# Where the latent attention starts beside the context's chain of work

## The chip, the cores and the metric

The kernel runs on one core of one Trainium2 chip. The metric is the device time of one execution, in microseconds (us). Five engines run side by side, each with its own instruction queue that is worked off in order: TensorE (PE, the matmuls; its weight loads are shown as PEld), VectorE (DVE), ScalarE (ACT), GpSimd (POOL) and SyncE (SP), which here issues nearly all DMAs.

## The reference

Two layers of a diffusion backbone work on 1024 latent tokens and 256 context tokens of width 1024. Layer 0 mixes by a short gated convolution and by differential attention, then applies one output projection; each layer ends in a gated ConvFFN. Context tokens read only context, latent tokens read both. What matters here is the second half of layer 0, cut to its core:

```python
y_lat = finish(gates_l, o_lat)                       # o_lat: attention of 1024 latent queries over 1280 keys
y_ctx = finish(gates_c, diff_attend(qc, kc, vc, lam))  # finish: concat(conv, attention) @ w_out
ctx = ctx + g1c * y_ctx                              # the context's output projection
ctx = ctx + g2c * conv_ffn(modulate(rms_norm(ctx, norm2_g[i]), sh2c, sc2c), ...)
```

`diff_attend` makes two softmax maps per head over the keys, subtracts the second times a factor from the first, and multiplies by v; the result is RMS-normalised per head. The context's output projection, norm and FFN need only context data; the latent attention needs q, k and v of layer 0. Neither needs the other.

## The kernel before

All matmuls of the gemm kind are done as three passes (high by high, high by low, low by high part) in `mm3` (lines 217 to 219). Weights come through `WStream`: a DMA into `wr`, a cast on ACT into `wh` (line 112), a subtraction on DVE into `wl` (line 114).

`attention` (line 1252 on) runs two generators side by side. The first, `chain`, is the context's tail of layer 0: one step that loads the mixed features (`mraw`, line 686) and splits them into `s4c`; eight steps of the output projection (PSUM tile `po`, 24 matmuls of 256 columns each, then `xc += gate * po` on DVE, line 696); two steps of `norm`; 22 `u` steps of the FFN's upper half (PSUM `pab`); and 24 `d` steps of its lower half (PSUM `pd`). The second, `att_lat`, is the latent attention: 4 heads by 2 halves of 512 queries make 8 blocks (`AttBlock`), numbered b0 to b7 below, of 4 query tiles each (q0 to q3). A query tile is three pieces: `scores` (twice, once per softmax map: six matmuls into the PSUM tile `S`, a maximum on DVE at line 1472, an exponential on ACT at line 1474 that reads `S`), `combine` (line 1487), and `product` (transposes `tpp`, line 1504, copies to `pth` and `ptl`, and for every second query tile the matmuls `pv`, whose result is written to `osq` and `osb`, lines 1514 and 1515). Two later pieces close a block: `stats` (column sums of `osq`, PSUM `ost`) and `out` (broadcast, `osb` scaled at line 1533 and stored at line 1534). `S` has one buffer, the PSUM tag `w` of `tpp`, `pv`, `ost` and `orb` two, the tag `mm` of the chain three.

`weave` takes steps of both generators in proportion to their planned number of steps. This gives the order of the program text. A planner then puts every engine's instructions into its queue ahead of the run: it goes by the order of the text where two instructions are ready, takes a later one where the earlier is not, and hands out the buffers of a tag when the tile is first written.

The tag `t2k` of the pool `tmp` (4 buffers of 512 columns) is shared by `mraw`, by the norm and by the attention:

```python
self.tmp = Pool(ctx.enter_context(tc.tile_pool(name="tmp", bufs=1)), {"t2k": ("t2k", 4)})
# norm, for k in range(8): squares; the first two stay as the two running sums
s = tmp.tile([P, 512], F32, tag="t2k", name="sq")[:, :T]
nc.scalar.activation(s, xk(k), AF.Square)
# norm, for k in range(8): the normed tile
t = keep(k) if keep else tmp.tile([P, 512], F32, tag="t2k", name="nt")[:, :T]
# AttBlock.__init__: both live until the block's `stats` and `out`
self.sq = net.tmp.tile([P, 512], F32, tag="t2k", name="osq")[:, :Q]
self.o = net.tmp.tile([P, 512], F32, tag="t2k", name="osb")[:, :Q]
```

`att_lat` makes the tiles of b0 at its start and those of block n+1 after `combine` of q2 of block n. The norm's squares are at lines 383 to 389, its column sum `st` at line 370, its reciprocal root at lines 357 and 359, its normed tiles `nt` at line 402.

Of the kernel before, what the change touches and what calls it, by code (L numbers as in the profile page):

```python
# [84 lines left out]
def weave(*gens):  # L85

    live = [[g, n, 0] for g, n in gens]
    while live:
        e = min(live, key=lambda e: (e[2] + 0.5) / e[1])
        if next(e[0], StopIteration) is StopIteration:  # L90
            live.remove(e)
        e[2] += 1
# [44 lines left out]
class Net:  # L137
# [1114 lines left out]
    def attention(self):  # L1252

        nc, tc, I = self.nc, self.tc, self.I
        B = self.modB
        with ExitStack() as s:
            cp = s.enter_context(tc.tile_pool(name="cp", bufs=1, reuse_waits="tile"))
            ap = s.enter_context(tc.tile_pool(name="ap", bufs=1, reuse_waits="tile"))
            pp = s.enter_context(tc.tile_pool(name="psS", bufs=1, space=PSUM, reuse_waits="tile"))
            xc = cp.tile([P, 8, CTX], F32, name="xc")  # L1260
            xk = lambda k: xc[:, k, :]
            s4c = lambda: cp.tile([P, 2, CTX], F32R, tag="s4c", name="s4c", bufs=14)
            tmp = self.tmp
            ps = Pool(pp, {"mm": ("mm", 3), "tp": ("mm", 3), "st": ("mm", 3)})

            def chain():
                op = self.out_proj(xk, CTX, SEQ, 1, self.mix, s4c, tmp, ps, lambda m, v: B[:, m, v:v + 1])
                next(op)
                nc.sync.dma_start(xc, I["ctxT"])
                yield  # L1270
                yield from op
                hs = []
                yield from self.norm(xk, CTX, self.gs[(0, 2, 1)], lambda k: B[:, 8 + k, 1:2], s4c, tmp, ps, hs, True)
                big = Pool(cp, {"a": ("a", 2), "b": ("b", 1), "cv": ("cv", 2), "e": ("e", 1)})
                yield from self.ffn(0, xk, CTX, hs, 4, s4c, big, ps, lambda m: B[:, 24 + m, 1:2])
                nc.sync.dma_start(self.xcD, xc)

            at = Pool(ap, {t: (t, 2) for t in ("k0", "k1", "vh", "vl", "qa0", "qa1", "qb0", "qb1", "s1", "p0", "p1",
                                               "e1", "r1")})
            pw = Pool(pp, {"w": ("w", 2), "S": ("S", 1)})  # L1280
            ch = chain()
            for _ in range(11):
                next(ch)
            weave((ch, 9 + 2 + 22 + 6 * 4 - 11), (self.att_lat(at, pw), 68))

    def rest(self, stop=99):
        nc, tc, I, O = self.nc, self.tc, self.I, self.O
# [364 lines left out]
```

## Time and profile before

| what | value |
|---|---|
| time, median of 3 runs | 2654.31 us (2648.61 to 2654.5) |
| the profiled execution: its own time | 2658.96 us |
| its span | 2657.2 us |
| PE busy | 2551.8 us, 96% of the span |
| DVE busy | 1947.5 us, 73% |
| ACT busy | 1166.3 us, 44% |
| granted TensorE clock, mean over the span | 0.974 |

Busy time of an engine is the union of its instructions. A matmul's row lasts longer than the time until the next one may start, because matmuls are pipelined: what a matmul takes of PE is read from start to start. A row of the timeline gives the start, the busy time, engine, line, operation, tiles and count, and in brackets the idle time just before it with what ended it. The granted clock is 1.00 at 2.4 GHz and 0.50 at 1.2 GHz.

### The profile page before, as it was taken

How to read it: one execution, taken by the hardware profiler on the slowest of the kernel's cores; microseconds unless marked ns; L12 is line 12 of the kernel's file. 1: busy time of each engine (PE TensorE's matmuls, PEld its weight loads, DVE VectorE, ACT ScalarE, POOL GpSimd, SP SyncE). 2: the span in 40 equal slices, each digit the busy share in tenths (PEclk: the TensorE clock that was granted, in tenths of full speed). 3: DMA queues.
4: the chain of work that ended last, by engine and by line, in shares of the span. 5: the costliest groups of instructions: out<-in, count | busy, mean ns of one | idle time of the engine just before them, and what ended most of it. 6: DMA issues, size and time to landing. Idle time of an engine off the chain costs nothing.

```text
span 2657.2 us, 34664 instructions
## 1 busy us (share of the span) xinstructions
PE 2551.8 (96%) x12666; PEld 2145.4 (81%) x12666; DVE 1947.5 (73%) x3077; ACT 1166.3 (44%) x1751; POOL 241.4 (9%) x321
## 2 busy tenths in 40 slices
PE   6999998999998998999999998999899999999999
PEld 6777887999997886888888886877688788888887
DVE  7467965999997587777778978446558766666984
ACT  5322324767675354444443454133235444444442
POOL 3221000000000041000000002013203100000000
PEclk6999999999999999999999999999799999999999
DMA  7224545443433624434458664577662222225874
GB/s 257 93 95 135 182 135 165 134 143 112 124 116 111 232 65 149 134 127 133 130 178 302 218 206 141 177 232 222 191 217 72 103 88 80 87 80 202 281 242 139
DMA packets 209547, 414.01 MB, mean 156 GB/s; under 512 B 20320, under 2 KB 89568, under 8 KB 208992
## 3 DMA queue, kind: packets, MB, share of 16 engines
q1 hardware_dynamic: 206352, 406.41, 46.6%
q10 hardware_dynamic: 3024, 5.38, 0.6%
q8 instruction: 99, 1.62, 0.3%
q14 instruction: 72, 0.59, 0.1%
HBM read 341.98 MB, written 69.73 MB: 155 GB/s over the span
## 4 chain that ended last, share of the span: by engine, by line
PE 63%; DVE 13%; issue 12%; DMA 7%; ACT 3%; POOL 2%; SPq 0%; ACTq 0%; DVEq 0%; POOLq 0%
PE PA L217 4%; PE PA L218 4%; PE PA L219 4%; PE pd L218 3%; PE pd L219 3%; PE pd L217 3%; PE PB L217 2%; PE PB L218 2%; PE PB L219 2%; PE pt L217 2%; PE pt L218 2%; PE pt L219 2%; PE po L218 2%; PE po L217 2%; PE po L219 2%
## 5 line engine op out<-in xcount | busy, mean ns | idle before, releaser
L114 DVE TENSOR_TENSOR wl<-wr,wh 128x1024 fp32r<-128x1024 f32 x254 | 309.6, 1221 | 178.4 <-ACT wh L112 176.1
L112 ACT CAST wh<-wr 128x1024 fp32r<-128x1024 f32 x254 | 261.9, 1034 | 394.1 <-PE PA L218 67.3
L217 PE MATMUL pd<-s,wh 128*128 128x512 f32 x616 | 241.2, 392 | 4.9 <-ACT s L963 4.9
L218 PE MATMUL pd<-s,wh 128*128 128x512 f32 x616 | 241.4, 392 | 1.8 <-DVE s L964 1.8
L219 PE MATMUL pd<-s,wl 128*128 128x512 f32 x616 | 241.1, 391 | 0.0
L217 PE MATMUL PA<-s,wh 128*128 128x512 f32 x544 | 212.2, 390 | 0.2 <-DVE a L893 0.2
L219 PE MATMUL PA<-s,wl 128*128 128x512 f32 x544 | 211.8, 389 | 0.0
L218 PE MATMUL PA<-s,wh 128*128 128x512 f32 x544 | 211.8, 389 | 0.0
L351 DVE SCALAR_TENSOR_TENSOR mw<-mw,cr 128x256 f32<-128x256 f32 x256 | 111.4, 458 | 81.3 <-DMA mw<-in_mod1T 71.9
L112 ACT CAST wh<-r 128x1024 fp32r<-128x1024 f32 x80 | 67.0, 837 | 220.6 <-PE PB L218 126.5
L217 PEld LDWEIGHTS pd<-s,wh 128*128 128x128 f32 x616 | 116.4, 189 | 29.4 <-ACT s L963 5.3
L218 PEld LDWEIGHTS pd<-s,wh 128*128 128x128 f32 x616 | 116.4, 189 | 27.2 <-DVE s L964 3.2
L219 PEld LDWEIGHTS pd<-s,wl 128*128 128x128 f32 x616 | 116.4, 189 | 24.2
L217 PE MATMUL PB<-s,wh 128*128 128x512 f32 x320 | 125.0, 390 | 1.2 <-ACT p L889 1.2
L218 PE MATMUL PB<-s,wh 128*128 128x512 f32 x320 | 124.8, 390 | 0.0
L219 PE MATMUL PB<-s,wl 128*128 128x512 f32 x320 | 124.6, 389 | 0.0
L217 PEld LDWEIGHTS PA<-s,wh 128*128 128x128 f32 x544 | 102.2, 188 | 22.3 <-DVE a L893 1.3
L219 PEld LDWEIGHTS PA<-s,wl 128*128 128x128 f32 x544 | 102.1, 188 | 21.2
L218 PEld LDWEIGHTS PA<-s,wh 128*128 128x128 f32 x544 | 102.2, 188 | 21.1
L1474 ACT ACTIVATE p<-S,s 128x1280 f32<-128x1280 f32 (+1 forms) x80 | 92.9, 1161 | 52.7 <-DVE s L1472 51.2
L359 POOL TENSOR_TENSOR rr<-vv,mhalf 128x8 f32<-128x8 f32 (+2 forms) x39 | 57.6, 1478 | 587.8 <-DVE vv L357 563.3
L1472 DVE TENSOR_REDUCE s<-S 128x1 f32<-128x1280 f32 (+1 forms) x80 | 102.0, 1275 | 11.1 <-PE S L1471 10.1
(385 smaller groups left out, 7000.3 us busy)
## 6 DMA issues: line engine op xcount, KB each, us to landing
wr<-in_w_up SPq DMA_DIRECT2D x98, 512.0 KB, 3.4
wr<-in_w_dn SPq DMA_DIRECT2D x92, 512.0 KB, 4.3
gr<-gD SPq DMA_DIRECT2D x154, 256.0 KB, 3.7
mw<-in_mod1T SPq DMA_DIRECT2D x256, 128.0 KB, 3.2
gD<-fcv SPq DMA_DIRECT2D x44, 512.0 KB, 3.6
wr<-in_w_out SPq DMA_DIRECT2D x40, 512.0 KB, 4.2
r<-in_w_up SPq DMA_DIRECT2D x40, 512.0 KB, 3.3
mbw<-in_mod0T SPq DMA_DIRECT2D x32, 512.0 KB, 3.6
```

What stands on the lines that cost most here:

```text
L112: self.nc.scalar.copy(hi, raw)
L114: eng.tensor_tensor(lo, raw, hi.bitcast(F32), op=ALU.subtract)
L217: mm(out, L[0], R[0], start=first, stop=False)
L218: mm(out, L[0], R[1], start=False, stop=False)
L219: self.last_mm = mm(out, L[1], R[0], start=False, stop=last)
L351: self.nc.vector.scalar_tensor_tensor(w, in0=w, scalar=1.0, in1=c, op0=ALU.mult, op1=ALU.mult, accum_out=d)
L359: self.last_pow = nc.gpsimd.tensor_tensor(r, vv, self.mhalf[:, :n], op=ALU.pow)
L1472: nc.vector.tensor_reduce(s2[:, m:m + 1], sv, axis=AX.X, op=ALU.max, negate=True)
L1474: nc.scalar.activation(e, sv, AF.Exp, bias=s2[:, m:m + 1], accum_out=self.s1[:, qt:qt + 1] if m == 0 else s2[:, 2:3])
```

## The change

The chain is no longer advanced by eleven steps (load, eight steps of output projection, two of the norm) before the weave begins, but by one (the load). The other ten steps become part of the weave, whose planned number of chain steps goes from 46 to 56. No instruction is added or removed.

```diff
             ch = chain()
-            for _ in range(11):
-                next(ch)
-            weave((ch, 9 + 2 + 22 + 6 * 4 - 11), (self.att_lat(at, pw), 68))
+            next(ch)
+            weave((ch, 9 + 2 + 22 + 6 * 4 - 1), (self.att_lat(at, pw), 68))
```

The order of the text that `weave` makes, by its rule (the generator whose next step lies earliest, (done + 0.5) / planned), begins as follows; A is a piece of the attention, C a step of the chain:

```
before: C load, C po0..po7, C norm1, C norm2, A scores b0q0, C u0, A combine b0q0, C u1, A scores b0q1, ...
        ... C u3, A product b0q1 + combine b0q2 + tiles of b1, A scores b0q3, C u4, ...
after:  C load, A scores b0q0, C po0, A combine b0q0, C po1, A scores b0q1, C po2, ...
        ... C po4, A product b0q1 + combine b0q2 + tiles of b1, A scores b0q3, C po5, ...
        ... C po7, A product b0q3 + combine b1q0, C norm1, A scores b1q1, A stats b0, C norm2, A scores b1q2, C u0,
        A out b0 + product b1q0 + product b1q1 + combine b1q2 + tiles of b2, C u1, ...
end, before: ... C d16-3, A scores b7q2, C u21, A out b6 ..., A scores b7q3, C d20-0, ...
end, after:  ... C d16-3, A out b6 ..., A scores b7q3, C u21, A combine b7q3, C d20-0, ...
```

## Rows read from the trace of the kernel before

**Rows 1.** The page, part 1: busy time, share of the span, instructions.
```profile
PE 2551.8 (96%) x12666; PEld 2145.4 (81%) x12666; DVE 1947.5 (73%) x3077; ACT 1166.3 (44%) x1751; POOL 241.4 (9%) x321
```
**Rows 2.** Windows, 425 to 862 us: stretch, length, busy by engine, clock, DMA.
```profile
425.00:450.00 25.00, 23.82 (x194) 23.56 (x195) 15.96 (x28) 12.43 (x24) 0.00 (x0) 1.00 0.79 208
450.00:475.00 25.00, 13.14 (x56) 10.78 (x55) 22.33 (x31) 16.22 (x26) 4.29 (x5) 0.59 0.57 171
...
480.00:800.00 320.00, 316.70 (x2428) 301.58 (x2427) 303.52 (x446) 224.31 (x391) 13.17 (x46) 1.00 0.40 124
820.00:850.00 30.00, 21.12 (x152) 18.83 (x150) 26.88 (x43) 17.57 (x31) 0.00 (x0) 0.98 0.25 90
850.00:862.00 12.00, 10.46 (x48) 8.96 (x47) 3.73 (x8) 2.76 (x6) 1.01 (x1) 0.64 0.61 206
```
**Rows 3.** Timeline of PE: output projection, norm, first FFN matmul.
```profile
425.51 0.62 PE L217 MATMUL po<-s4c,wh 128*128 128x256 f32 x3 [1.21 <-ACT s4c L688]
...
449.45 0.28 PE L219 MATMUL po<-s4c,wl 128*128 128x256 f32 x1
...
457.06 1.02 PE L370 MATMUL st<-ones,sq 128*128 128x1 f32 x4 [6.17 <-DVE sq L389]
...
466.41 0.79 PE L1470 MATMUL S<-k,qa 128*128 128x512 f32 x1 [5.57 <-ACT p L1474]
467.27 0.58 PE L217 MATMUL pab<-s4c,wh 128*128 128x256 f32 x1
```
**Rows 4.** Timeline of ACT: exponentials of b7, little chain work left.
```profile
823.56 1.34 ACT L1474 ACTIVATE p<-S,s 128x1280 f32<-128x1280 f32 x1
...
828.03 1.33 ACT L1474 ACTIVATE p<-S,s 128x1280 f32<-128x1280 f32 x1 [0.94 <-DVE s L1472]
...
843.00 1.33 ACT L1474 ACTIVATE p<-S,s 128x1280 f32<-128x1280 f32 x1
```
**Rows 5.** Timeline of PE: matmuls of one query tile.
```profile
836.65 0.33 PE L217 MATMUL pv<-pth,vh 128*128 128x256 f32 x1
...
840.12 0.39 PE L1470 MATMUL S<-k,qa 128*128 128x512 f32 x1
...
841.27 1.03 PE L1504 MATMUL tpp<-ident,p 128*128 128x128 f32 x8
```
**Rows 6.** Tile sq in 420:470, and timeline of DVE: the norm.
```profile
L383 ACT ACTIVATE sq<-xc x8: 405/414/418, 435.0 to 453.4; 128x256 f32<-128x256 f32 x8
L388 DVE TENSOR_TENSOR sq<-sq x6: 416/418/427, 437.1 to 455.1; 128x256 f32<-128x256 f32 x6
...
456.58 0.42 DVE L389 TENSOR_TENSOR sq<-sq 128x256 f32<-128x256 f32 x1
```
**Rows 7.** Timelines of ACT and SP, tile osb: the end of block b7.
```profile
856.49 0.38 ACT L1514 ACTIVATE osq<-pv 128x256 f32<-128x256 f32 x1 [5.70 <-PE pv L219]
...
860.85 0.33 SPq L1534 DMA_DIRECT2D mix<-osb  x1
...
DMA to landing us min/median/max: 1.7/2.1/3.6
```
**Rows 8.** Timeline of SP, tile kraw, timeline of DVE: the first head.
```profile
429.10 1.09 SPq L666 DMA_DIRECT2D kraw<-kT  x2
...
DMA to landing us min/median/max: 3.8/4.9/7.4
...
438.77 1.49 DVE L669 TENSOR_TENSOR k<-kraw,k 64x1280 fp32r<-64x1280 f32 x1
```
**Rows 9.** Timeline of PE at the end of the attention.
```profile
847.26 1.06 PE L1504 MATMUL tpp<-ident,p 128*128 128x128 f32 x8 [2.26 <-DVE p L1487]
```
**Rows 10.** Timeline of SP before the output projection: its first loads.
```profile
360.12 0.33 SPq L1534 DMA_DIRECT2D mix<-osb  x1
...
371.33 10.04 SPq L588 DMA_DIRECT2D mix<-cv  x2
...
382.89 8.39 SPq L686 DMA_DIRECT2D mraw<-mix  x3
```

## The prediction

> **What bounds the kernel now.** I read the page first: PE is busy for 2551.8 of 2657.2 us, DVE for 1947.5 [rows 1]. A busy PE can still be a waiting one, so the second view is the windows over the stage that the change touches, 425 to 862 us. From 480 to 800 us, where attention and FFN are woven, PE is busy for 316.70 of 320 us at the full clock, and DVE for 303.52 [rows 2]. PE idles 3.3 us there, 1%, so this stretch ends when PE's work ends; DVE at 95% has little room, but it is second. The two ends are different. From 425 to 475 us PE idles 1.2 + 11.9 = 13.1 us, and the granted clock falls to 0.59 in the second half [rows 2]. From 820 to 850 us PE idles 8.9 us while DVE is busy for 26.88 of 30 [rows 2].
>
> Third, PE's timeline shows what the first hole is. The eight output projections run without a hole from 425.51 to 449.45 us; then PE waits 6.17 us for the norm's sum and 5.57 us for the first exponentials, and the first FFN matmul starts at 467.27 [rows 3]. A matmul of S already stands in this hole: the planner pulls the attention's start forward by itself. The hole costs more than its idle time. A mean clock of 0.59 over 25 us means that some 20 us ran at the 1.2 GHz level; of the 13.14 us that PE worked in this half about 10 lay in it and at full clock would have taken 5. So the opening costs 13.1 + 5 = 18 us of PE time. That is all that the change can win there.
>
> **The change part by part.** No instruction comes or goes, on any queue. What moves is the attention against ten steps of the chain, and the DMAs that they issue: kraw, qraw and vraw of b0 and b1 are now ahead, on SP, of the weights of the later output projections. In the trace the first kraw goes out at 429.10, right behind the mraw loads, and its landing takes 3.8 to 7.4 us [rows 8]. It can hardly go earlier, because the mraw loads stay first. With 4.9 us of landing, the cast, and 1.49 us for the split on DVE [rows 8], S of b0q0 starts near 438 instead of 449.6, and b0q1's first exponential, after the second key tile has gone through the single kraw buffer, near 452. What is pushed back on SP is weights, 0.3 us each in the queue and prefetched two ahead; I cost it at nothing, and with that cover gone at one landing, for which kraw's 4.9 us is the nearest row [rows 8].
>
> The output projection is 192 matmuls in 449.45 - 425.51 = 23.9 us [rows 3]. It now shares PE with about one and a half query tiles and is through near 455.
>
> **The step that decides is the norm's buffers.** The tag t2k has four. The text now has b0's osq and osb, then b1's, then the norm's eight squares, its eight nt, and then b2's. I take it that a tag's buffers are given in the order of the text, a later tile never before an earlier one. The trace bears this out weakly: after the last block but one of the context's attention is stored at 360.12, SP has spare time, yet the first mraw loads go out only at 382.89 [rows 10], when the last block's osq and osb, earlier in the text, are about to be written. If it holds, the squares wait until b1's osq and osb have been given, at b1q1's product. The first two squares then take b0's buffers and stay there as the running sums, so the third square waits until `stats` of b1 has read osq. Until then the whole chain stands still: no FFN, and only attention on PE.
>
> How long? Alone, the attention goes at the pace of the one S buffer: reduce, exponential, next matmuls. Exponentials at 823.56 and 828.03 are 4.47 us apart; over four half tiles to 843.00 it is 19.44 / 4 = 4.86 [rows 4]. I take 4.7, so 9.4 us for a query tile. From b0q1's first exponential at 452 to b1q3's second are 13 half tiles, 61 us: 513. From the last exponential to the written osq the end of b7 took 856.49 - 843.00 = 13.5 us [rows 4, 7]; with part of that at the low clock I take 13: 526. Six squares through one free buffer, each 0.41 us on ACT and 0.42 on DVE [rows 6], some 0.95 with the hand-overs: 6 us, 532. From the last sum at 456.58 to the first FFN matmul at 467.27 are 10.7 us [rows 3, 6]: 543. osb of b1, stored 4.4 us after osq and landed 2.1 us later [rows 7], comes inside that. b2's osq needs a buffer only at about 545, so no second wait follows.
>
> So PE has attention alone from 455 to 543, 88 us. One query tile takes 2 x (841.27 - 840.12) = 2.3 us for S, 10 transposes at 1.03 / 8, 1.3 us with their tail (1.1 without), half of 840.12 - 836.65 for pv, 1.7 [rows 5], and 0.3 for a quarter of a block's sums and broadcasts: 5.4 to 5.6, I take 5.4. PE then idles 88 x (1 - 5.4 / 9.4) = 37 us. The lower bound takes 4.47 a half tile and a start 6 us earlier, 75 us: 75 x (1 - 5.4 / 8.9) = 29. The upper takes 4.86 and a start later by 4, 95 us: 95 x (1 - 5.4 / 9.7) = 42. At the opening itself the 1.2 us stays. I expect no low clock in this stretch, as the mean clock was 0.98 from 820 to 850 us with holes of this kind [rows 2].
>
> Against 18 - 1 = 17 us lost before at this place, 37 us are 20 more, with the bounds 12 to 25. Afterwards the chain is behind and is served first; PE stays full, as it was, and DVE has slightly less than before per unit of PE work, so nothing is lost there; won is at best the 1% of the stretch that PE idles now, 3 us, at least 0. I take 2, as the chain's matmuls are always ready while it is behind.
>
> At the end of the weave u21 comes two places later, beside b7q3's combine. Its 48 matmuls of 256 columns take 48 x 0.125 = 6 us, from 23.9 / 192 a piece [rows 3], and can fall into PE's holes there: 8.9 us in 820 to 850, and such a one as the 2.26 us ahead of b7q3's transposes [rows 2, 9]. I take 5 of the 6 as won; bounds 0 and 6.
>
> Sum: +20 for the stall against the old hole, -5 for the end, -2 for the catching up: +13 us on the profiled execution's 2658.96 (its span and 1.8 us around it), which is 4.65 above the median of the runs. On the median: 2654.31 + 13 = 2667 us. With the bounds, 12 - 6 - 3 = +3 and 25 us, so the likeliest's own range is 2658 to 2679.
>
> The Trainium skill (Perfetto Trace Analysis, Optimization Strategy) says that a kernel with several regimes may gain when they are interleaved; by that alone the change would win the opening's idle time, the case of the first rival. The same section says that the same gap repeating on the engine that should be saturated can mean that there is no SBUF for the next tile. No run here shows such a stretch yet: PE idles 1% of 480 to 800 us [rows 2].
>
> **The rivals.** First, on the other side: the squares get buffers when their data is there, whatever the text says, and b0's osq waits a little instead. Then the norm ends near 475 with attention beside it, PE loses some 8 us in place of 18 (the 1.2 at the start, one wait of the 6.17 kind cut to half, and some low clock), and u21 wins 3 of its 6: 2654 - 10 - 3 = 2641, or 2635 to 2648. For it: the planner moves ready work ahead, as the S matmul in the norm's hole shows [rows 3]. Against: mraw's late start [rows 10]. It decides if the squares' first rows on ACT stand before b1's first osq. Chance 0.16.
>
> Second, the change does not do what it says: the planner already starts the attention at 429.10 as soon as it can [rows 8], so the queues hardly change and so does the time, 2654. Against: the squares' wait follows from the text, not from readiness. It also covers a stall whose 29 us are nearly met by 18 + 7 won. Chance 0.14.
>
> Third, the stall also lowers the clock: PE idles 43% of it, and in the opening 12 us of idle time in 25 were enough for a clock of 0.59 [rows 2]. At half rate S takes 1.15 us more per half tile, 8 query tiles 18 us more: 2685. Against: 0.98 from 820 to 850 us, with 30% idle [rows 2]. Chance 0.10.
>
> **How the numbers follow.** Forecast 0.60, rivals 0.16, 0.14, 0.10. A measurement of this kernel tells about 0.3%, 8 us, from no change. Of the forecast 0.46 lies above +8 us and 0.14 below; the first rival gives 0.14 faster and 0.02 same, the second 0.12 same and 0.01 on either side, the third 0.10 slower. Together slower 0.57, same 0.28, faster 0.15. The range runs from 2641, the middle of the first rival, to 2682, leaving out half of it, most of the third and the forecast's tails, under 2 in 10.
>
> **What would show it.** Right: S of b0q0 some 10 us earlier; the squares, now done by 453.4 [rows 6], in two groups, the third after b1's first ost matmuls, past 500; the first pab near 543 instead of 467; from 455 to 543 PE busy near 57%, with a clock of 1.00; four query tiles more done at 543 than before; fewer idle us on PE in the last 40 us of the weave. Wrong: the first pab before 490 (first rival), the order on PE unchanged (second), a clock well under 1 between 455 and 543 (third), or PE idle time in the later weave well over 1%, which would mean that the catching up is not free.

## The result: 1% slower, and the profile after

| | before | after |
|---|---|---|
| time, median | 2654.25 us (2648.61 to 2654.5, 4 runs) | 2680.18 us (2670.85 to 2682.11, 4 runs) |
| the profiled execution: its time, span | 2658.96, 2657.2 us | 2680.5, 2678.6 us |

The ratio is 1.0096, 95% interval 1.0069 to 1.0123: 18 to 33 us slower. The forecast said 2667, so the sign was right, the time lies inside the range, and the loss is twice the one forecast. From the line of `exp` on, lines of the kernel after have numbers one lower than before (L1473 for L1474).

Part 1 of the page, for [rows 1]:

```profile
PE 2558.1 (96%) x12666; PEld 2150.0 (80%) x12666; DVE 1948.8 (73%) x3077; ACT 1165.5 (44%) x1751; POOL 236.4 (9%) x321
```

The counts are the same, so nothing was added. PE is busy 6.3 us longer for the same matmuls, and the span grew by 21.4. To see where, take the stage from the first matmul of the context's output projection to the first of the latent one, which is the same work in both kernels. The windows of before over that stage (stretch, length, busy time of PE, PEld, DVE, ACT, POOL, clock, DMA):

```profile
425.50:859.70 434.20, 407.93 (x3063) 386.52 (x3063) 391.60 (x576) 288.02 (x497) 20.38 (x53) 0.97 0.42 130
425.50:480.00 54.50, 41.96 (x290) 39.34 (x291) 41.44 (x62) 31.16 (x52) 4.29 (x5) 0.81 0.69 194
...
800.00:859.70 59.70, 49.26 (x349) 45.60 (x347) 46.65 (x70) 32.55 (x55) 2.92 (x2) 0.94 0.32 107
```

And of after:

```profile
426.40:888.00 461.60, 419.71 (x3062) 393.67 (x3063) 395.23 (x576) 287.33 (x497) 15.16 (x53) 0.94 0.40 123
426.40:550.00 123.60, 91.62 (x576) 82.04 (x577) 91.91 (x129) 68.92 (x116) 5.08 (x10) 0.81 0.41 118
...
450.00:475.00 25.00, 13.53 (x58) 10.60 (x57) 20.80 (x23) 13.37 (x18) 0.00 (x0) 0.71 0.72 204
475.00:500.00 25.00, 18.18 (x104) 15.28 (x103) 20.46 (x25) 14.27 (x25) 0.00 (x0) 0.81 0.29 81
500.00:525.00 25.00, 11.98 (x52) 9.51 (x51) 16.09 (x30) 11.92 (x25) 4.05 (x5) 0.60 0.00 1
525.00:550.00 25.00, 25.00 (x189) 24.30 (x188) 17.77 (x28) 16.72 (x31) 1.03 (x6) 0.92 0.29 95
550.00:820.00 270.00, 268.06 (x2063) 255.28 (x2061) 249.48 (x365) 182.91 (x320) 7.99 (x41) 1.00 0.41 126
...
820.00:888.00 68.00, 60.04 (x429) 56.34 (x428) 53.83 (x84) 35.50 (x64) 2.09 (x4) 0.92 0.35 117
```

The stage is 461.6 - 434.2 = 27.4 us longer: 41.9 us of idle PE instead of 26.3, which is 15.6, and 419.7 us of busy PE instead of 407.9 for the same 3063 matmuls, which is 11.8. Most of the second part is the clock. A mean of 0.94 over 461.6 us is about 55 us at the half level; 0.97 over 434.2 was about 26. Added up over the stretches at 0.50, PE is busy for 36 us of them in after and for 17 in before; at the full clock this work would take half, so the clock accounts for about 9.5 of the 11.8 us. This is an estimate, and the other 2 us are not traced. The loss lies in the opening; from 550 to 820 us PE idles 1.9 us of 270, less than the 3.3 of 320 in [rows 2]. This stage's 27.4 fits the 26 us between the medians. The profiled spans differ by only 21.4, because outside the stage, where both kernels do the same, the profiled execution of before took 6.0 us longer; its time is 4.7 us above its own median.

PE's timeline in the opening, for [rows 3] (start, busy time, ..., in brackets the idle time ahead and what ended it):

```profile
426.40 0.61 PE L217 MATMUL po<-s4c,wh 128*128 128x256 f32 x3 [1.22 <-ACT s4c L688]
...
452.65 0.28 PE L219 MATMUL po<-s4c,wl 128*128 128x256 f32 x1
...
502.75 0.95 PE L370 MATMUL ost<-ones,osq 128*128 128x1 f32 x8
...
516.33 1.02 PE L370 MATMUL st<-ones,sq 128*128 128x1 f32 x4 [1.92 <-DVE sq L389]
518.37 0.69 PE L375 MATMUL rb<-ident,rr 128*128 128x128 f32 x2 [1.03 <-POOL rr L359]
...
522.86 0.79 PE L217 MATMUL pab<-s4c,wh 128*128 128x256 f32 x2 [3.81 <-ACT s4c L413]
...
532.21 0.60 PE L375 MATMUL orb<-ident,r 128*128 128x128 f32 x4
```

The projection ends 3.2 us later than before, as it shares PE. The first FFN matmul comes at 522.86 instead of 467.27: 70 us behind the last projection matmul, where it was 18. ACT's timeline, for [rows 6], shows why:

```profile
442.89 1.33 ACT L1473 ACTIVATE p<-S,s 128x1280 f32<-128x1280 f32 x1 [1.72 <-DVE s L1471]
...
453.87 1.32 ACT L1473 ACTIVATE p<-S,s 128x1280 f32<-128x1280 f32 x1
...
459.54 1.32 ACT L1473 ACTIVATE p<-S,s 128x1280 f32<-128x1280 f32 x1
...
482.63 0.47 ACT L1514 ACTIVATE osb<-pv,subg 128x256 f32<-128x256 f32 x1
482.99 0.72 ACT L383 ACTIVATE sq<-xc 128x256 f32<-128x256 f32 x2
...
503.79 0.42 ACT L383 ACTIVATE sq<-xc 128x256 f32<-128x256 f32 x1 [1.26 <-PE ost L370]
...
510.44 1.33 ACT L1473 ACTIVATE p<-S,s 128x1280 f32<-128x1280 f32 x1 [2.00 <-DVE s L1471]
...
512.68 0.42 ACT L383 ACTIVATE sq<-xc 128x256 f32<-128x256 f32 x1 [0.51 <-DVE sq L388]
...
536.41 1.31 ACT L1473 ACTIVATE p<-S,s 128x1280 f32<-128x1280 f32 x1
```

Not one square of the norm runs until b0's `osb` has been written at 482.63; then two run in the same microsecond, and the third stands until `ost` of b0 has read `osq`. The bracket names that reader. That is a wait for a buffer: the squares' data was there, since the last projection ended at 452.65. The rows also show something else: the exponentials stop for 26 us between 510.44 and 536.41.

What ended PE's idle time in this stretch, by groups of lines from 450 to 525 us (count, busy us and mean ns, idle time ahead and its releasers):

```profile
L1469 PE MATMUL S<-k,qa 128*128 128x512 f32 (+1 forms) x33 | 16.7, 505 | 16.3 <-ACT p L1473 16.2
L1503 PE MATMUL tpp<-ident,p 128*128 128x128 f32 x40 | 8.3, 354 | 7.1 <-DVE ptl L1505 4.1 <-DVE p L1486 3.0
...
L217 PE MATMUL pab<-s4c,wh 128*128 128x256 f32 x3 | 1.2, 470 | 3.8 <-ACT s4c L413 3.8
```

Of 31 us, 16.3 are S waiting for the exponential that frees its buffer and 7.1 the transposes: attention alone on PE, limited by its own circle over DVE and ACT. The cause of the stall does not stand in this table. It shows what is left to do for PE while the chain is kept out, and the missing work has no row.

At the end ([rows 7]), ACT's timeline has b7's `osq` at 884.89 instead of 856.49:

```profile
884.89 0.38 ACT L1513 ACTIVATE osq<-pv 128x256 f32<-128x256 f32 x1 [5.53 <-PE pv L219]
```

### The profile page after: what moved, and what is told of

It reads as the page before. It is cut to its first block, busy times and chain, and to the rows that moved or that the text cites. A ratio compares the mean times of both kernels' runs of the same rounds, so it can differ in the third digit from the quotient of the medians.

```text
span 2678.6 us, 34650 instructions
## 1 busy us (share of the span) xinstructions
PE 2558.1 (96%) x12666; PEld 2150.0 (80%) x12666; DVE 1948.8 (73%) x3077; ACT 1165.5 (44%) x1751; POOL 236.4 (9%) x321
## 4 chain that ended last, share of the span: by engine, by line
PE 62%; DVE 13%; issue 12%; DMA 7%; ACT 4%; POOL 2%; ACTq 0%; SPq 0%; DVEq 0%; POOLq 0%
PE PA L218 4%; PE PA L217 4%; PE PA L219 4%; PE pd L218 3%; PE pd L219 3%; PE pd L217 3%; PE PB L217 2%; PE PB L218 2%; PE PB L219 2%; PE pt L217 2%; PE pt L219 2%; PE pt L218 2%; PE po L218 2%; PE po L217 2%; PE po L219 2%
## 5 line engine op out<-in xcount | busy, mean ns | idle before, releaser
L218 PEld LDWEIGHTS pd<-s,wh 128*128 128x128 f32 x616 | 116.3, 189 | 26.3 <-DVE s L964 2.2
L1473 ACT ACTIVATE p<-S,s 128x1280 f32<-128x1280 f32 (+1 forms) x80 | 92.8, 1160 | 67.5 <-DVE s L1471 65.0
L219 PEld LDWEIGHTS PA<-s,wl 128*128 128x128 f32 x544 | 102.1, 188 | 21.1
```

What stands on the lines that cost most here:

```text
L218: mm(out, L[0], R[1], start=False, stop=False)
L219: self.last_mm = mm(out, L[1], R[0], start=False, stop=last)
L1473: nc.scalar.activation(e, sv, AF.Exp, bias=s2[:, m:m + 1], accum_out=self.s1[:, qt:qt + 1] if m == 0 else s2[:, 2:3])
```

## The experiments

The theory: the chain is kept out by the four `t2k` buffers, that is all, and with buffers of its own the change would win what it looked for. The rival that came from the trace: the order ties do it as well. `in_order` (line 362) issues the norm's and the attention's small matmuls (`st`, `rb`, `ost`, `orb`) behind the last gemm matmul that stands ahead of them in the text. With the chain woven in, that is a matmul of the other generator.

Line numbers in a run's rows are those of its own kernel. In each entry the time behind "against" is that of the kernel before, measured beside the run. The stage is the time from the first context `po` to the first latent `po` in the profiled execution, as above: 434.2 us before, 461.6 after. A single execution of it tells no difference of 5 us: the two controls below, as fast as before by their medians, have 436.4 (c1) and 439.5 (c2).

**Own buffers for the norm (e1_own).** The pool of the chain gets two more `cv` buffers, which the norm uses ahead of the FFN; a small class `NormTmp`, not shown, turns the norm's tag `t2k` into this one. Control c1_before_own: the same edit in the kernel before.

```diff
-  yield from self.norm(xk, CTX, ..., s4c, tmp, ps, hs, True)
-  big = Pool(cp, {..., "cv": ("cv", 2), ...})
+  yield from self.norm(xk, CTX, ..., s4c, NormTmp(cp, tmp), ps, hs, True)
+  big = Pool(cp, {..., "cv": ("cv", 4), ...})
```

> Theory (buffers): the change loses because the norm's squares wait for the four t2k buffers behind b0's osq and osb. With four buffers of the chain's own for the norm, the squares are done before 465 us, the first pab starts before 490 instead of 523, PE idles under 15 us from 450 to 525 (changed kernel: some 31), and the time is 2635 to 2650 us, below before's 2654. Rival (order): what costs is that the attention's loads and DVE work now lie ahead of the projections' weights, whatever the buffers; then the time stays at 2670 to 2682 us.

> Control: the kernel before, with the norm's own buffers. By the theory (buffers) the norm never waits there, since it ends ahead of b0's osq: 2651 to 2657 us. If four buffers for the FFN's tile of the same tag, or the other addresses, were a gain in themselves, it would be 5 us or more faster, and the first run would have to be read against it.

Measured: 2671.34 us (6 runs) against 2659.12, ratio 1.0052 (1.0034 to 1.0070); stage 450.4. Control 2658.86, 0.9996 (0.9985 to 1.0007). So the buffers are part of the loss and not the whole of it; the theory alone falls: `pab` comes at 512.3 and not before 490. The time lies in the range of the rival (order), which e4 below takes up. What is left stands in the answer for the tile `sq` of e1 (count, shortest, median and longest ns, first and last start):

```profile
L395 ACT ACTIVATE sq<-xc x8: 407/418/419, 438.1 to 459.6; 128x256 f32<-128x256 f32 x8
...
L401 DVE TENSOR_TENSOR sq<-sq x1: 405/405/405, 470.5 to 470.5; 128x256 f32<-128x256 f32 x1
```

And in PE's timeline of e1:

```profile
504.75 0.28 PE L231 MATMUL pv<-pth,vl 128*128 128x256 f32 x1
504.87 0.50 PE L382 MATMUL st<-ones,sq 128*128 128x1 f32 x4
...
512.33 0.79 PE L229 MATMUL pab<-s4c,wh 128*128 128x256 f32 x2 [1.18 <-ACT s4c L425]
```

All eight squares are through by 460 and the sum is complete at 470.9, yet its column sum `st` runs at 504.87, directly behind the last `pv` of b0q3, with no idle time between. b0q3's product stands ahead of the norm in the text, and `st` is tied to its last matmul. A second wait had stood behind the first, 34 us long.

**The tie of the attention's own sums taken away (e2_free), and both (e3_both).** `stats` and `out` issue their matmuls without `in_order` (the edit in `stats`; `out` has its counterpart, not shown):

```diff
-  net.colsum(st, self.sq, n)
+  for j in range(n):
+      nc.tensor.matmul(st[:, j:j + 1], self.sq[:, j * P:(j + 1) * P], net.ones, start=True, stop=True)
```

> The attention's sums and broadcasts (ost, orb) are no longer tied behind the last gemm matmul of the text. Theory (tie): in the changed kernel b0's orb waits behind u0 of the stalled chain, and with it the PSUM tag w, so that the attention stands still from 511 to 535 us too; without the tie its exponentials go on through 511 to 535 and the time falls by 6 to 12 us to 2668 to 2674, the first pab staying near 523. Rival (buffers alone): the attention stands still because of the buffers of t2k; then the gap of 26 us between two exponentials stays and the time stays at 2676 to 2682 us.

> Both edits together. If the buffers are the root and the tie only carries the stall on, this stands within 4 us of the run with the norm's own buffers alone (2635 to 2650 us). If the tie costs something of its own all along the weave, it is 5 us or more below that run. If the order of loads is what costs, it stays above 2665.

Measured: e2 2683.29 us (4 runs), 1.0100 (1.0079 to 1.0121), stage 460.0; e3 2671.84 (7 runs), 1.0046 (1.0030 to 1.0062), stage 445.8. The expected gain of e2 is a miss. e3 stands with e1 and not at 2635 to 2650; above 2665, it too leaves the order of the loads open. PE's timeline of e2:

```profile
509.13 1.11 PE L1533 MATMUL orb<-ident,r 128*128 128x128 f32 x4 [2.40 <-POOL r L1527]
```

And the exponentials in ACT's, from 507 to 532 us:

```profile
507.61 1.33 ACT L1473 ACTIVATE p<-S,s 128x1280 f32<-128x1280 f32 x1 [0.37 <-DVE s L1471]
...
514.68 1.33 ACT L1473 ACTIVATE p<-S,s 128x1280 f32<-128x1280 f32 x1
...
522.82 1.33 ACT L1473 ACTIVATE p<-S,s 128x1280 f32<-128x1280 f32 x1
...
530.78 1.33 ACT L1473 ACTIVATE p<-S,s 128x1280 f32<-128x1280 f32 x1 [0.44 <-DVE s L1471]
```

Here the exponentials go on to 530.8, since `orb` no longer waits behind the FFN's first gemm; the stop from 510 to 536 in after came from this tie. It cost nothing, though: without it `pab` comes at 528.9, 6 us later than in after, and once the chain is free PE is full with or without attention.

**Own buffers and no tie at all (e4_own_untied), no tie alone (e5_untied).** Within `attention()` `in_order` gives no edge. Control c2_before_own_untied: both edits in the kernel before.

```diff
-  return self.tc.issue_after(self.last_mm.ins) if self.last_mm else nullcontext()
+  return self.tc.issue_after(self.last_mm.ins) if self.last_mm and self.tie else nullcontext()
...
+  n.tie = False
   n.attention()
+  n.tie = True
```

> The norm's own buffers, and no tie to the last gemm matmul of the text in attention and chain during the weave. Theory (two waits): with own buffers the squares were done at 460 us, but the column sum st came at 505, because it is tied behind the last matmul of the text, b0q3's pv. Without the tie st comes before 475, the first pab before 490, PE idles under 15 us from 450 to 525 and the time is 2635 to 2654 us, not slower than before. Rival (order): the attention beside the projections costs by itself, in the weave and at its end; then st and pab come early and the time still stays at 2662 us or more.

> The changed kernel without the tie alone, t2k still shared. Theory (two waits): the third square still waits for b0's osq to be read, near 503 us, so the stall stays: first pab at 515 to 530, time 2674 to 2686 us. If the tie were the only wait that counts, the first pab would come before 490 and the time fall below 2660.

> Control: the kernel before with the norm's own buffers and without the tie. Both theories: the norm's sum follows the projections there anyway, so 2651 to 2662 us, within 4 us of before in the same call. If it were 6 us or more faster, a gain of the untied version with the change would belong to the tie, not to the place of the attention.

Measured: e4 2660.92 us (12 runs) against 2656.94, 1.0009 (0.9998 to 1.0019), stage 438.1; e5 2681.58 (6 runs), 1.0090 (1.0073 to 1.0107), stage 455.6; control 2657.32, 1.0003 (0.9991 to 1.0014). Without the tie but with shared buffers the loss is that of after: the third square still waits for `ost` (ACT's timeline of e5):

```profile
505.34 0.42 ACT L384 ACTIVATE sq<-xc 128x256 f32<-128x256 f32 x1 [1.25 <-PE ost L371]
```

With both waits away the loss is gone but for at most 5 us, by the interval of e4. `st` before 475 and `pab` before 490 came as expected; the time came neither in the theory's range (up to 2654) nor in the rival's (from 2662), so the order of the text can still cost a little, and it is not what cost the 26 us. So there are two waits in series. The buffer's ends later: taking it alone away wins some 12 us, taking the tie alone away nothing that these runs tell, and only both win it, within those 5 us. Nothing is won over before either. PE's timeline of e4:

```profile
467.59 0.50 PE L383 MATMUL st<-ones,sq 128*128 128x1 f32 x4
...
483.35 0.50 PE L230 MATMUL pab<-s4c,wh 128*128 128x256 f32 x2 [1.44 <-ACT s4c L426]
```

And its windows:

```profile
450.00:475.00 25.00, 14.36 (x69) 11.89 (x68) 20.92 (x27) 15.34 (x22) 2.00 (x1) 0.80 0.56 151
475.00:500.00 25.00, 20.96 (x115) 17.95 (x116) 21.94 (x33) 17.42 (x33) 4.00 (x4) 0.80 0.28 67
...
820.00:850.00 30.00, 24.96 (x186) 22.78 (x185) 26.35 (x38) 19.20 (x32) 0.00 (x0) 1.00 0.39 132
```

From 450 to 500 us PE idles 10.6 + 4.0 = 14.7 us and runs 20 us at the half level (a mean clock of 0.80 over 50 us). Before it was 11.9 + 0.6 = 12.4 us idle and the same 20 us at the half level. The hole was not filled, it was spread: the first FFN matmul comes at 483 instead of 467, and attention alone does not fill PE until then. From 820 to 850 us 8.9 us of idle time ([rows 2]) become 5.0, but e4 is some 4 us later there; up to the end of the stage, from 800 us on, it is 9.3 instead of 10.4.

Why `pab` comes so late with nothing to wait for stands in DVE's timeline of e4:

```profile
460.08 0.75 DVE L401 TENSOR_TENSOR sq<-sq 128x256 f32<-128x256 f32 x2
...
463.29 1.49 DVE L1484 TENSOR_REDUCE s<-S 128x1 f32<-128x1280 f32 x1 [1.32 <-PE S L1483]
...
466.97 0.41 DVE L402 TENSOR_TENSOR sq<-sq 128x256 f32<-128x256 f32 x1
```

The norm's partial sums are ready at 460.8, but their total runs at 466.97: in DVE's queue it stands behind a weight split and the attention's maximum and copies, and for 1.32 us DVE even waits for an S. The projection ends only 2.8 us later than before (452.2), but from there to `pab` it is 31 us instead of 18, with DVE busy for 21 to 22 of each 25 us.

**Only the norm woven (e6_nine), and that with both waits away (e7_nine_own_untied).**

```diff
-  next(ch)
-  weave((ch, 9 + 2 + 22 + 6 * 4 - 1), (self.att_lat(at, pw), 68))
+  for _ in range(9):
+      next(ch)
+  weave((ch, 9 + 2 + 22 + 6 * 4 - 9), (self.att_lat(at, pw), 68))
```

> Half of the change: nine steps of the chain (load and eight projections) ahead of the weave, only the norm woven in; shared t2k and tie as they are. The text then has the norm ahead of b0's first product, so neither wait can arise. Theory (two waits): the first pab stays before 480 us, time 2648 to 2660 us, as before. Rival (order): the more attention stands ahead of the FFN in the text, the slower; two of the ten steps' worth of it would show as 2660 to 2668 us.

> The kernel after with nine chain steps ahead of the weave (the load and all eight output projections), so that only the norm's two steps are woven, with the norm's temporaries in buffers of the chain's own and without the order tie of norm and attention. The version that the runs point to as the best candidate: the output projection keeps PE full until 449 as before, and the norm neither waits for the attention's buffers nor for its matmuls. Theory (the hole of some 18 us in 450 to 475 us is the norm's own latency, some 30 us from the last projection to the first FFN matmul, and attention alone fills PE to a little over half): the first pab comes at 467 to 475, time as before within 5 us, 2652 to 2662. Rival (the weave of the projection was what spread the hole, and with the tie gone attention fills the hole as far as it is ready): first exponential before 450, PE idle in 450 to 475 under 9 us instead of 12.4, clock above 0.8, time 2645 to 2651.

Measured: e6 2656.31 us (12 runs) against 2656.94, 0.9996 (0.9986 to 1.0006), stage 430.9; e7 2656.44 (12 runs) against 2658.61, 0.9997 (0.9986 to 1.0007), stage 432.8. e7's rival misses. PE's timeline of e7:

```profile
458.76 1.01 PE L383 MATMUL st<-ones,sq 128*128 128x1 f32 x4 [4.64 <-DVE sq L402]
...
472.56 1.28 PE L230 MATMUL pab<-s4c,wh 128*128 128x256 f32 x3
```

And its window:

```profile
450.00:475.00 25.00, 14.65 (x66) 12.33 (x65) 22.51 (x33) 18.05 (x30) 4.39 (x5) 0.69 0.67 191
```

With the norm's two steps woven in and no buffer or tie shared, the hole stays: 10.4 us idle, a clock of 0.69, `pab` at 472.6. It is the time of the norm, squares, sum, root, broadcast and normed tiles, 20 us from the last projection to the first FFN matmul, beside an attention that alone cannot fill PE. It is not all the norm's own latency, though: DVE is still shared, and busy for 22.5 of these 25 us. The traces let this be compared over the norm's second half, from the start of `st` to the first `pab`:

| | after | e1 | before | e2 | e7 | e4 |
|---|---|---|---|---|---|---|
| from `st` to `pab`, us | 6.5 | 7.5 | 10.2 | 10.4 | 13.8 | 15.8 |
| of it DVE busy with work that is not the norm's, us | 0.0 | 4.5 | 4.1 | 3.2 | 8.0 | 11.5 |

In after the attention stood still just then. In the main, the more of the attention's work and of the weight splits falls between, the longer the norm takes. So the attention that is to fill the hole also makes it longer. This compares runs that were made for something else; none puts the norm's instructions ahead on DVE.

e6 also says that shared buffers and tie do not hurt when the norm's steps come in the text ahead of b0's products: with the norm near the weave's start, `st` runs at 455.7 and `pab` at 468.9. No version beats the kernel before by more than the measurement tells.

## Why the prediction was right, and where its sizes were off

- **The earlier start.** S of b0q0 was to start some 10 us earlier. Its first exponential is at 442.9, 12 us earlier than before (455.3). Right. b0q0 has a second one, for its second map, at 453.87; the first of b0q1, forecast near 452, is the third, at 459.54, so the stall's clock started 7.5 us late. The projection ends at 452.65 (forecast near 455).
- **The norm's buffers decide.** Right, by the order of the squares in after, and by e1 and e5. Two squares behind b0's `osb`, the third after an `ost`, past 500 us: as forecast.
- **Which block ends the stall.** Wrong: the third square came after `ost` of b0, at 503.8, not of b1. The step "the squares wait until b1's osq and osb have been given" failed. A tag's buffers are handed out when a tile is first written, as the description of the kernel says. b1's first `osq` is written in b1q1's product, which stands behind both norm steps in the order of the text that the prediction itself listed. So the chain came back at 522.9 instead of 543.
- **The pace of the attention alone.** From 453.87 to 510.44 the exponentials take 56.6 us for ten half tiles, 5.7 each where 4.7 was taken. Much of this stretch ran at the half clock, where S takes longer: its matmuls of 512 columns start 0.43 us apart from 506.97 on, and 0.23 from 501.59 on. How much of the pace this explains is not shown. By the forecast's pace `osq` of b0 would have been written near 489; it was at 501.8. So b0 ended later than the forecast would have it, and this partly made up for the wrong block. That is luck.
- **The clock.** "I expect no low clock in this stretch" failed. The four windows from 450 to 550 us have 0.71, 0.81, 0.60 and 0.92: 48 us at the half level, where before had 20. The 0.98 of 820 to 850 us in [rows 2] was the wrong row to go by; the 0.59 of 450 to 475 in the same group was the right one, and the row right behind the 0.98, 850 to 862 us, has 0.64. The third rival had the mechanism and priced it at 18 us; the stage's busy time grew by 11.8, some 9.5 of it by the clock.
- **The sum.** The opening was to cost 37 us of idle time and no clock, against 12 idle and 5 of clock: +25 of idle time and -5 of clock, +20. Measured, PE idles 32.0 us until 550 instead of 12.5 until 480, +19.4, and the busy time, instead of falling by 5, grew by 11.8 in the stage. The idle term was too high by some 5, over a stall of 70 us instead of 88. The end was to win 5 by u21: idle time after the weave's full stretch is 8.0 us (820 to 888) instead of 10.4 (800 to 859.7), so 2.5. Catching up was to win 2: 1.9 us idle instead of 3.3, so 1.4. 19.4 - 2.5 - 1.4 = 15.5 of idle time, and 11.8 of busy time: 27.3, where the forecast had 25 - 5 - 2 = 18 of idle time and -5 of clock, 13. The mis-sized term is the clock in the stall.
- **The other signs.** From 455 to 523 us PE is busy for 58%, as forecast (57%), but at a clock of 0.69 and not 1.00. At 543 one query tile more is done than before (14 exponentials against 12), not four. In the last 40 us of the stage PE idles 8.0 us instead of 10.4, as forecast.
- **The tie.** Not seen at all. It would have held the norm until b0q3's last `pv`, 504.9 in e1, even with buffers for everyone. So the first rival (the squares get buffers when their data is there, 2641) could not have come true: e1, where they do, is 14 us slower than before. The forecast was right partly by luck: the wait it named ended later than the one it missed, `st` at 516.3 in after against 504.9 in e1.
- **What can be won.** "18 us of PE time" for the hole was a bound and not a gain. e4, with no such wait left, wins none of it.

Left open: how much of the 14.7 us of idle time in e4 would go if the norm did not share DVE's queue with the attention, and what a second buffer for S would do for an attention that is alone on PE; no run has either.

## What to carry to other kernels

Before weaving two chains of work earlier, list what they share: buffer tags (in order of the first write) and explicit edges of order that name "the last matmul", whichever chain it belongs to. When one wait is taken away, look at what stands right behind it, since two in series each hide the other's price. And a hole on the bounding engine is worth its idle time only if the filler can fill it: here the filler was a latency-bound circle of its own that used the same DVE as the norm, and the hole was spread, not closed.

## What was not expected of the hardware

The clock. In after, 48 us out of 450 to 550 ran at 1.2 GHz, while PE was at work for 13.5, 18.2 and 12.0 us of each 25 in the first three windows, without one idle stretch on PE over 4 us (the longest took 3.81). Before, from 820 to 850 us, PE worked for 21.1 of 30 us and had 0.98. What that does to a matmul is seen in the groups of lines by shape (count, busy us and mean ns, idle time ahead), of after from 450 to 525 us:

```profile
L1469 PE MATMUL S<-k,qa 128*128 128x512 f32 x22 | 12.8, 581 | 16.3 <-ACT p L1473 16.2
```

And of before from 820 to 850 us, with the same kind of wait ahead:

```profile
L1470 PE MATMUL S<-k,qa 128*128 128x512 f32 x9 | 3.8, 426 | 3.7 <-ACT p L1474 3.7
```

581 ns instead of 426 for the same matmul. So here the stall of the bounding engine cost more than the time in which it did nothing: some 9.5 us by the clock (the estimate above) on top of 15.6.
